# Pool-weight fold one group per block, gate in the output stage, rings set apart, and the next modulation block behind two of six product groups, in a conditioned hybrid layer on one core

## The chip, the cores and the metric

One Trainium2 chip, of which the kernel uses one core. The metric is the device time of one execution in microseconds (us); the numbers shown are single runs and their median.

## The reference

The layer takes x of 4096 tokens by 1024 and a conditioning vector c of 1024, all in float32:

```python
mod = silu(c) @ w_ada + b_ada
shift, scale, gate = split(mod, 3, axis=-1)
h = layer_norm(x) * (1.0 + scale) + shift
proj = h @ w_in + b_in                       # 1024 -> 2560
u_a, z_a, glu_b, z_b = proj[..., :512], proj[..., 512:1024], proj[..., 1024:2048], proj[..., 2048:]
pooled = causal_multiscale_pool(u_a)         # windows 2, 4, 8, 16, one per group of 128, minus u itself
y_a = (einsum("bsgc,gcd->bsgd", pooled, w_pool) + b_pool) * ls_pool * silu(z_a)
v = glu_b[..., :512] * sigmoid(glu_b[..., 512:])
v = silu(layer_norm(causal_depthwise_conv(v, w_dw, b_dw)) * ln_conv_g + ln_conv_b)   # 31 taps
y_b = (v @ w_pw + b_pw) * silu(z_b)
y = concat(y_a, y_b) @ w_out + b_out
out = layer_norm(ALPHA * x + gate * y) * ln_post_g + ln_post_b
```

Since the pooling is linear in the channels' place, `w_pool` (times `ls_pool`) can be multiplied into the u columns of `w_in`: this is the *fold*. It is four products of a 128 x 1024 slice of transposed `w_in` with a 128 x 128 group of `w_pool`.

## The kernel before

**The products.** TensorE does each float32 product as three (`mm3`, lines 336 to 339): both operands are split into a high and a low part (`split`, ScalarE casts the high part, VectorE subtracts for the low one), and high x high, high x low and low x high are added up in PSUM. A product is 128 weight columns by 512 tokens. Tokens are worked in eight *blocks* of 512 (`sb` 0 to 7); a *chunk* is 128 columns of `w_in`, and its product over the 1024 rows (k = 0 to 7) takes 24 instructions.

**Phase 1** (lines 461 to 498) makes for each block the eight GLU chunks 8 to 15, two by two (`glus`), and the z chunks 16 and 17 (`z_half`). Its input is xT, x transposed, normalised, scaled and shifted, as high and low part. While block sb is worked, xT of block sb + 1 is prepared: `row_stats` loads four tiles of 128 tokens, takes mean and variance with two ScalarE scans each (lines 265 and 267), transposes the eight columns of statistics on TensorE (`xcp`), copies them to a row (`rowsx`, line 275), writes them to DRAM (`rD`) and reads them back spread over the partitions (`xbc`). `norm_T` loads the transposed x (`xk`, two k at a time) and applies the statistics and the scale on VectorE (lines 292 and 294); `mod_xT` makes the high part on ScalarE (line 303) and the low part on VectorE (line 304) and writes both to DRAM (`xD`). Phase 2 reads them back for the z_a chunks 4 to 7, the u chunks 0 to 3 (with the folded weights) and the chunks 18 and 19. The x tiles, `xbc` and the `xk` tiles share a ring of five buffers, "tm".

**Block 0** is different (lines 374 to 439). Its x is transposed on TensorE (`turn_x`), and its scale and shift come straight from the modulation. `w_ada` is loaded in five pieces; `mod_block` multiplies each into `macc` on VectorE (line 181), adds it up over the partitions on TensorE (line 186) and makes the scale and shift of one or two k. For each k, a row of 128 x 1024 of `w_in` is loaded (`load_row`) and split in two goes (`split_cols`, three column chunks and one), x is made (`mod_turned`, lines 321 to 324), then come the modulation block and the transposes of the next k, and then the products of k for six chunks at once, the *six product groups*: 8, 12, 9, 13, 10, 14. `load_row` keeps its rows in two "wraw" buffers and in the homes of `gate_bc` and `gbo`, which are not filled yet.

**The fold** (`fold_u`, lines 350 to 364) comes after the z chunks of block 0, all four groups one after the other. Each loads `wT` (512 KB), makes eight 128 x 128 products into two PSUM banks (`fv`), copies them out (`wf`), writes them to DRAM (`uD`), and folds the bias (`bu`). `wT` and `wf` use the two "wraw" buffers. The gate (`mod_gate` and lines 490 to 498, eight loads of 512 KB and eight VectorE operations of 1024 columns, two products) comes after block 1.

**The convolution** (`conv`, 31 taps on VectorE, lines 558 to 586) is written after phase 2 but has no place of its own: VectorE's order has its taps between the other steps. The order of each engine is set by a scheduler before the run, from priorities and estimated times; at run time each engine takes its instructions strictly in that order. So does SP, which issues nearly all the DMAs: a load whose buffer isn't free holds up all that stand behind it. After the phases comes the output stage: pointwise product, `w_out` scaled by the gate, and the last layer norm.

Of the kernel before, what the change touches and what calls it, by code (L numbers as in the profile page):

```python
# [17 lines left out]
P = 128  # L18
# [21 lines left out]
def tile_layer(ctx, tc, x, x_t, w_in_t, c, w_ada, b_ada, w_in, b_in, w_pool, b_pool, ls_pool, w_dw, b_dw,  # L40
# [132 lines left out]
    def mod_block(b, k0, nk, wts):  # L173
        w = nk * P
        acc = s2.tile([P, 2, w], F32, tag="bc", bufs=2, name=f"macc_{b}", padded_shape=[P, 2, DH])
        last = None
        for kt in range(KT):
            if kt == 0:
                nc.vector.tensor_scalar(acc, wts[kt], sc[:, 0:1], None, op0=ALU.mult)
            else:  # L180
                last = nc.vector.scalar_tensor_tensor(acc, wts[kt], sc[:, kt : kt + 1], acc,
                                                      op0=ALU.mult, op1=ALU.add)
        ps = tp_bank(f"mod{b}")
        for i in range(2):
            for j in range(nk):
                nc.tensor.matmul(ps[:, nk * i + j : nk * i + j + 1], acc[:, 1 - i, j * P : (j + 1) * P],
                                 ones[:, 0:1], start=True, stop=True)
# [69 lines left out]

    def load_x(i):
        xt = ph.tile([P, D], F32, tag="tm", bufs=5, name=f"x{i}")
        nc.sync.dma_start(xt, tok(xv, i))  # L260
        return xt

    def col_stats(src, n, nmean, rstd, name):
        sm = st.tile([P, 3], F32, tag="sm", bufs=4, name=f"sm{name}")
        nc.scalar.activation(src, src, AF.Identity, accum_out=sm[:, 0:1])  # L265
# [5 lines left out]
    def to_rows(pb, cs, dst, name):  # L271
        n = cs.shape[1]
        transpose(pb[:n, :P], cs)
        rows = st.tile([n, P], F32, tag="rows8", bufs=2, name=f"rows{name}", padded_shape=[4 * TT, P])
        nc.scalar.copy(rows, pb[:n, :P])
        nc.sync.dma_start(dst, rows)

    def row_stats(sb):
        cs = st.tile([P, 8], F32, tag="cs", bufs=2, name=f"xcs{sb}")
        for t in range(TT):  # L280
            i = sb * TT + t
            xt = load_x(i)
            col_stats(xt, D, cs[:, t : t + 1], cs[:, 4 + t : 5 + t], f"x{i}")
# [3 lines left out]
        return bc  # L287

    def norm_T(sb, bc, k):
        z = ph.tile([P, 2, T], F32, tag="tm", bufs=5, name=f"xk{sb}_{k}")  # L290
        nc.sync.dma_start(z, x_t[k * P : (k + 2) * P, sb * T : (sb + 1) * T].rearrange("(k p) s -> p k s", p=P))
        nc.vector.tensor_tensor(z, z, bc[:, 0:1, :].to_broadcast([P, 2, T]), op=ALU.add)  # L292
# [56 lines left out]

    def fold_u(g, wpl):  # L350
        wT = wraw(f"wT{g}")
        nc.sync.dma_start(wT, w_in_t[g * P : (g + 1) * P, :])
        wf = wraw(f"wf{g}")
        for hb in range(2):
            pb = s2_bank(f"fv{g}_{hb}")
            for j in range(4):
# [4 lines left out]
        nc.sync.dma_start(uD[g], wf)  # L361
        pb = s2_bank(f"bu{g}")
        nc.tensor.matmul(pb[:, 0:1], wpl[:, g, :], vec("b_in", g), start=True, stop=True)
# [25 lines left out]
    def load_row(k):  # L389
        home = k % 4  # L390
        rows[k] = (wraw(f"wr{k}") if home < 2 else
                   cst.tile([P, D], F32, tag=("gate", "gbo")[home - 2], name=f"wr{k}"))
        nc.sync.dma_start(rows[k], w_in[k * P : (k + 1) * P, 8 * P : 16 * P])

# [6 lines left out]

    def split_cols(k, m0, m1):
        split(*(t.rearrange("p (h c) -> p h c", h=2)[:, :, m0 * P : m1 * P] for t in (*Wg[k], rows[k])))

# [30 lines left out]
    gate_bc = cst.tile([P, D], F32, tag="gate", name="gate_bc")  # L435
    gbo = cst.tile([P, D], F32, tag="gbo", name="gbo")
    for k in range(KT):
        for i in range(2):
            after(nc.sync.dma_start(xD[k][0][:, i, :], xT[k][i].bitcast(F32)), last, True)

    def glu(sb, m, pa, pg):
# [19 lines left out]
    for sb in range(NSB):  # L461
# [13 lines left out]
        xT_next = mod_xT(sb + 1, zs, 0)  # L475
        zs = norm_T(sb + 1, bc, 4) + norm_T(sb + 1, bc, 6)
        z_half(sb, xT)
        xT = xT_next + mod_xT(sb + 1, zs, 4)
        if sb == 0:
            wpl = s2.tile([P, MC, P], F32, tag="cto", bufs=2, name="wpl")  # L480
# [4 lines left out]
            nc.vector.tensor_tensor(bpl, vec("b_pool", 0, 4), vec("ls", 0, 4), op=ALU.mult)  # L485
            for g in range(MC):
                fold_u(g, wpl)
        if sb == 1:
            mod_gate(gbo)
            gb = wraw("gb")  # L490
            nc.sync.dma_start(gb, b_ada[2 * D : 3 * D].partition_broadcast(P))
            for h in range(2):
                sl = slice(h * 512, (h + 1) * 512)
                gp = tp_bank(f"gp{h}")
                nc.tensor.matmul(gp, ones, gbo[:, sl], start=True, stop=True)
                nc.vector.tensor_tensor(gate_bc[:, sl], gp, gb[:, sl], op=ALU.add)
            nc.sync.dma_start(gbo, b_out.partition_broadcast(P))
            nc.vector.tensor_tensor(gbo, gbo, gate_bc, op=ALU.mult)
# [13 lines left out]
    for sb in range(NSB):  # L512
# [188 lines left out]
    def out_tile(sb, t, ys):  # L701
# [104 lines left out]
```

## Time and profile before

| what | us |
|---|---|
| runs | 1396.62, 1403.74, 1404.29 |
| median | 1403.74 |
| the profiled execution | 1397.84 |
| its span | 1395.8 |
| TensorE busy in it | 1356.4 (97%) |
| VectorE busy | 1193.9 (86%) |
| ScalarE busy | 432.6 (31%) |

A row of a timeline gives start, duration, engine, line, operation, output and inputs, shape, the count of instructions run together, and in brackets how long the engine had been idle before it and what ended that. Times are in us from the start of the span. PE is TensorE, DVE is VectorE, ACT is ScalarE, SPq the queue of SP. The granted clock is the share of full speed that TensorE had.

### The profile page before, as it was taken

To read this page: it belongs to the slowest core of one execution; us is meant where nothing else is said; L and a number is where in the kernel's file an instruction comes from. 1 tells how busy PE (TensorE), PEld (TensorE's weight loads), DVE (VectorE), ACT (ScalarE), POOL (GpSimd) and SP (SyncE) were. 2 spreads that over 40 slices of the span, in tenths; PEclk is the share of its full clock that TensorE was granted. 3 is DMA by queue.
4 is the path that set the end of the run, shared out by engine and by line. 5 is a ranking of instruction groups with operands and counts; after the bars stand their busy time and mean duration, and the time that the engine had idled before them with its cause. 6 is when DMAs were issued, how large, how long until landed. Compare 5 with 4: busy or idle time off the path is not lost.

```text
span 1395.8 us, 17137 instructions
## 1 busy us (share of the span) xinstructions
PE 1356.4 (97%) x6045; PEld 1118.5 (80%) x6045; DVE 1193.9 (86%) x2348; ACT 432.6 (31%) x772; POOL 131.0 (9%) x193
## 2 busy tenths in 40 slices
PE   4898999999999999999999999999999999999997
PEld 3777888888888888888888888888888888888886
DVE  8688989983569999899899699999997899998754
ACT  3544235245531231411114111343234131322310
POOL 1000000010100001210111110100111101001111
PEclk9999999999999999999999999999999999999999
DMA  9958677477563662360541723466444443433511
GB/s 323 328 180 323 214 275 267 163 267 235 180 249 124 226 194 83 131 233 23 182 139 59 234 67 123 131 203 196 157 167 148 139 159 118 162 129 130 186 61 76
DMA packets 113352, 243.81 MB, mean 175 GB/s; under 512 B 15027, under 2 KB 45555, under 8 KB 113267
## 3 DMA queue, kind: packets, MB, share of 16 engines
q1 hardware_dynamic: 103984, 209.15, 43.4%
q0 software_dynamic: 9216, 33.56, 7.2%
q8 instruction: 47, 0.77, 0.2%
q14 instruction: 39, 0.31, 0.1%
q10 hardware_dynamic: 66, 0.02, 0.0%
HBM read 156.65 MB, written 86.04 MB: 174 GB/s over the span
## 4 chain that ended last, share of the span: by engine, by line
PE 90%; DMA 5%; DVE 2%; ACT 2%; SPq 1%; issue 1%; DVEq 0%; ACTq 0%
PE po L713 25%; PE p L338 6%; PE p L339 6%; PE p L337 6%; PE p2z L338 4%; PE p2u L338 4%; PE p2z L337 4%; PE p2z L339 4%; PE p2u L337 4%; PE p2u L339 4%; PE pw L689 2%; PE pw L691 2%; PE pw L690 2%; PE p2b L338 2%; PE p2b L337 2%; PE p2b L339 2%
## 5 line engine op out<-in xcount | busy, mean ns | idle before, releaser
L576 DVE SCALAR_TENSOR_TENSOR cx<-cv,wdw,cx 128x513 f32<-128x513 f32 (+1 forms) x240 | 145.7, 613 | 0.7
L576 DVE SCALAR_TENSOR_TENSOR ca<-cx,wsum,ca 128x256 f32<-128x256 f32 (+1 forms) x240 | 143.7, 611 | 0.1
L576 DVE SCALAR_TENSOR_TENSOR ca<-cv,wdw,ca 128x256 f32<-128x256 f32 (+1 forms) x224 | 134.3, 611 | 0.0
L742 POOL TENSOR_TENSOR ors<-ove,mhalf 128x1 f32<-128x1 f32 x32 | 46.9, 1467 | 408.8 <-DVE ove L738 400.4
L736 ACT ACTIVATE ojk<-r,osm 128x1024 bf16<-128x1024 f32 x31 | 35.6, 1148 | 148.3 <-DVE osm L733 148.3
L332 POOL DMA_DIRECT2D x2r<-xD x64 | 34.8, 544 | 402.8 <-PE p2b L339 276.7
L731 DVE SCALAR_TENSOR_TENSOR r<-po,r 128x512 f32<-128x512 f32 x62 | 40.9, 687 | 22.0 <-PE po L713 21.9
L576 DVE SCALAR_TENSOR_TENSOR lx<-lv,wdw,lx 128x257 f32<-128x257 f32 x120 | 57.5, 479 | 0.0
L576 DVE SCALAR_TENSOR_TENSOR la<-lx,wsum,la 128x256 f32<-128x256 f32 x120 | 57.3, 478 | 0.0
L576 DVE SCALAR_TENSOR_TENSOR la<-lv,wdw,la 128x256 f32<-128x256 f32 x112 | 53.3, 478 | 0.0
L269 POOL TENSOR_TENSOR xcs<-smx,mhalf 128x1 f32<-128x1 f32 x28 | 20.7, 740 | 343.9 <-DVE smx L268 343.6
L517 ACT ACTIVATE sz<-p2z,cols 128x512 f32<-128x512 f32 x32 | 22.0, 688 | 95.6 <-PE p2z L339 95.5
L292 DVE TENSOR_TENSOR xk<-xk,xbc 128x1024 f32<-128x1024 f32 x28 | 34.1, 1222 | 17.2 <-DMA xk<-in_x_t_dram 17.2
L303 ACT ACTIVATE x<-xk,shc 128x512 fp32r<-128x512 f32 x56 | 38.0, 719 | 31.5 <-DVE xk L294 31.5
L304 DVE SCALAR_TENSOR_TENSOR x<-xk,shc,x 128x512 fp32r<-128x512 f32 x56 | 40.4, 749 | 8.3 <-ACT x L303 8.3
L524 ACT ACTIVATE u<-p2u,bu 128x512 f32<-128x512 f32 x32 | 22.0, 689 | 70.4 <-PE p2u L339 70.4
L745 DVE SCALAR_TENSOR_TENSOR r<-r,ors,b_bc 128x1024 f32<-128x1024 f32 (+1 forms) x33 | 41.1, 1248 | 3.2 <-POOL ors L742 3.1
L443 ACT ACTIVATE sg<-p,cols 128x512 f32<-128x512 f32 x32 | 21.9, 686 | 70.3 <-PE p L339 69.8
L265 ACT ACTIVATE x<-x 128x1024 f32<-128x1024 f32 x28 | 29.6, 1059 | 40.6 <-DMA x<-in_x_dram 39.7
L713 PE MATMUL po<-wo0h,ya 128*128 128x512 f32 x128 | 41.2, 392 | 0.0
L713 PE MATMUL po<-wo1h,ya 128*128 128x512 f32 x128 | 41.1, 390 | 0.0
L705 DVE SCALAR_TENSOR_TENSOR r<-r,gbo 128x1024 f32<-128x1024 f32 x32 | 39.0, 1218 | 1.7 <-DMA r<-in_x_dram 1.7
(360 smaller groups left out, 4107.4 us busy)
## 6 DMA issues: line engine op xcount, KB each, us to landing
x2r<-xD POOLq DMA_DIRECT2D x64, 512.0 KB, 7.3
xD<-x SPq DMA_DIRECT2D x56, 512.0 KB, 5.4
x<-in_x_dram SPq DMA_DIRECT2D x32, 512.0 KB, 6.8
r<-in_x_dram SPq DMA_DIRECT2D x32, 512.0 KB, 3.6
out_dram<-r SPq DMA_DIRECT2D x31, 512.0 KB, 2.6
xk<-in_x_t_dram SPq DMA_DIRECT2D x28, 512.0 KB, 8.2
wa<-in_w_ada_dram SPq DMA_DIRECT2D x32, 256.0 KB, 6.4
vD<-v SPq DMA_DIRECT2D x32, 256.0 KB, 2.2
```

The lines of the kernel that those rows point to most:

```text
L303: nc.scalar.activation(h2[:, 0, :], z, AF.Identity, bias=shc[:, k : k + 1])
L304: nc.vector.scalar_tensor_tensor(h2[:, 1, :], z, shc[:, k : k + 1], h2[:, 0, :].bitcast(F32), op0=ALU.add, op1=ALU.subtract)
L337: nc.tensor.matmul(ps, w[0], X[0], start=first, stop=False)
L338: nc.tensor.matmul(ps, w[0], X[1], start=False, stop=False)
L339: nc.tensor.matmul(ps, w[1], X[0], start=False, stop=last)
L576: nc.vector.scalar_tensor_tensor(dst, src, wt, dst, op0=ALU.mult, op1=ALU.add)
L705: xg = nc.vector.scalar_tensor_tensor(r, r, ALPHA, gbo, op0=ALU.mult, op1=ALU.add)
L713: mm = nc.tensor.matmul(po[h], lhs, Wo[k][wi][:, h * 512 : (h + 1) * 512], start=(k == 0 and wi == 0 and lhs is yh), stop=last)
L731: nc.vector.scalar_tensor_tensor(r[:, sl], po[h], 1.0, r[:, sl], op0=ALU.mult, op1=ALU.add, accum_out=sm[:, h : h + 1])
L736: nc.scalar.activation(jk, r, AF.Square, bias=sm[:, 2:3], accum_out=ss)
L742: nc.gpsimd.tensor_tensor(rs, ve, mhalf[:, 0:1], op=ALU.pow)
L745: nc.vector.scalar_tensor_tensor(r[:, sl], r[:, sl], rs, b_bc[:, sl], op0=ALU.mult, op1=ALU.add)
```

## The change

It has six parts.

1. The fold is done one group per block, after blocks 2 to 5, each with its `wT` loaded one block earlier. `wpl` (`w_pool` times `ls_pool`) is prepared after block 1 in the program's text. The folds use the PSUM banks of transposes ("tpb") in place of "s2b", and `wf` lies in the ring "tm".
2. The gate is written in phase 2, after block 2 of it (`GATE_SB`), and `gate_bc` and `gbo` are made only after phase 1.
3. The x tiles for the statistics leave the ring "tm": the four of block 1 are loaded early into "ca" buffers, those of later blocks go by turns into the two homes of `gate_bc` and `gbo`. The writes of block 0's xT to `xD` come after the last `xk` load of block 1 instead of after the last modulation block.
4. `load_row` loads three of the four column chunks of either half; chunks 11 and 15 are loaded behind (`w3r`, eight loads of 128 x 256) and split on their own. The high part of a row is cast before x is made, the low part after. `wzr` goes from "wraw" to the homes of the gate.
5. The modulation block and transposes of the next k come behind two of the six product groups.
6. The rings `sm` and `rows8` are split in one for x and one for the convolution; `bs` has three buffers instead of four.

```diff
-        sm = st.tile([P, 3], F32, tag="sm", bufs=4, name=f"sm{name}")
+        sm = st.tile([P, 3], F32, tag=f"sm{name[0]}", bufs=4, name=f"sm{name}")
...
-        rows = st.tile([n, P], F32, tag="rows8", bufs=2, name=f"rows{name}", padded_shape=[4 * TT, P])
+        rows = st.tile([n, P], F32, tag=f"rows{name[0]}", bufs=1, name=f"rows{name}", padded_shape=[4 * TT, P])
...
-            xt = load_x(i)
+            xt = x_early[t] if sb == 1 else load_x(i, t % 2)
...
-    def fold_u(g, wpl):
-        wT = wraw(f"wT{g}")
-        nc.sync.dma_start(wT, w_in_t[g * P : (g + 1) * P, :])
-        wf = wraw(f"wf{g}")
+    def fold_u(g, wpl, wT):
+        wf = ph.tile([P, D], F32, tag="tm", bufs=5, name=f"wf{g}")
         for hb in range(2):
-            pb = s2_bank(f"fv{g}_{hb}")
+            pb = tp_bank(f"fv{g}_{hb}")
...
     for k in range(KT):
+        hi, lo = (both(t)[:, :, : 3 * P] for t in Wg[k])
+        nc.scalar.copy(hi, rows[k])
         xT.append(mod_turned(pb, k))
-        split_cols(k, 0, 3)
-        split_cols(k, 3, 4)
-        if k + 1 < KT:
-            if k + 1 in starts:
-                b = starts[k + 1]
-                last = mod_block(b, *mods[b], wad[b])
-            pb = turn_x(xt_next, k + 1)
-        for n0, ps in zip(first, pss0):
+        nc.vector.tensor_tensor(lo, rows[k], hi.bitcast(F32), op=ALU.subtract)
+        for i, (n0, ps) in enumerate(zip(first, pss0)):
+            if i == 2 and k + 1 < KT:
+                if k + 1 in starts:
+                    b = starts[k + 1]
+                    last = mod_block(b, *mods[b], wad[b])
+                pb = turn_x(xt_next, k + 1)
             mm3(ps, W[n0][k], xT[k], k == 0, k == KT - 1)
+    for q in range(2):
+        raw = wraw(f"w3r{q}").rearrange("p (k h c) -> p k h c", k=4, h=2)
+        for k in range(4):
+            nc.sync.dma_start(raw[:, k], both(w_in[(4 * q + k) * P : (4 * q + k + 1) * P, 8 * P : 16 * P])[:, :, 3 * P :])
+        for k in range(4):
+            hi, lo = (both(t)[:, :, 3 * P :] for t in Wg[4 * q + k])
+            split(hi, lo, raw[:, k])
...
+        if sb == 0:
+            for k in range(KT):
+                for i in range(2):
+                    after(nc.sync.dma_start(xD[k][0][:, i, :], xT[k][i].bitcast(F32)), x_loads[1])
         z_half(sb, xT)
         xT = xT_next + mod_xT(sb + 1, zs, 4)
-        if sb == 0:
+        if sb == 1:
...
-            for g in range(MC):
-                fold_u(g, wpl)
-        if sb == 1:
-            mod_gate(gbo)
...
+        if 1 <= sb <= MC:
+            wT = wraw(f"wT{sb - 1}")
+            nc.sync.dma_start(wT, w_in_t[(sb - 1) * P : sb * P, :])
+        if 2 <= sb <= MC + 1:
+            fold_u(sb - 2, wpl, wTs.pop(0))
+        if 1 <= sb <= MC:
+            wTs.append(wT)
...
+        if sb == GATE_SB:
+            mod_gate(gbo)
```

Three places show how the order of instructions moves. The first is TensorE at the end of the z chunks of block 0 (`p1z_1`), before; `fv` and `bu` are the fold, `p_1_8` and the like the products of block 1 for chunk 8 with x of k = 0, `x_1_0`.

```order
L339 MATMUL p1z_1_1016<-x_0_7_741,wz1l 128x512
L358 MATMUL fv_0_1069<-wpl,wT_1066 128x128 x4
L358 MATMUL fv_1_1075<-wpl,wT_1066 128x128 x4
L363 MATMUL bu_1082<-cols,wpl 128x1
L337 MATMUL p_1_8_1192<-x_1_0_962,wg0h 128x512
L337 MATMUL p_1_12_1193<-x_1_0_962,wg0h 128x512
L337 MATMUL p_1_9_1247<-x_1_0_962,wg0h 128x512
L337 MATMUL p_1_13_1248<-x_1_0_962,wg0h 128x512
L358 MATMUL fv_0_1088<-wpl,wT_1085 128x128 x4
L358 MATMUL fv_1_1094<-wpl,wT_1085 128x128 x4
L363 MATMUL bu_1101<-cols,wpl 128x1
L358 MATMUL fv_0_1107<-wpl,wT_1104 128x128 x4
```

The same place of the changed kernel, where lines 344 to 346 are the three products; `xcp_1101` transposes statistics of block 2.

```order
L346 MATMUL p1z_1_1024<-x_0_7_736,wz1l 128x512
L74 MATMUL xcp_1101<-ident,xcs_1068 8x128
L344 MATMUL p_1_8_1118<-x_1_0_954,wg0h 128x512
L344 MATMUL p_1_12_1119<-x_1_0_954,wg0h 128x512
L344 MATMUL p_1_9_1173<-x_1_0_954,wg0h 128x512
L345 MATMUL p_1_8_1118<-x_1_0_954,wg0h 128x512
L346 MATMUL p_1_8_1118<-x_1_0_954,wg0l 128x512
L345 MATMUL p_1_12_1119<-x_1_0_954,wg0h 128x512
```

The folds are gone from here: three products with x's high part follow the z chunks, and the fourth is the first that reads its low part.

The second place is VectorE between the first normalising operation of block 1 (`xk_0`, line 292, some rows above these) and the low half of `x_1_0` (line 304), before; lines 570 to 576 are the convolution.

```order
L292 TENSOR_TENSOR xk_4_978<-xk_4_978,xbc_880 128x1024
L294 SCALAR_TENSOR_TENSOR xk_0_882<-xk_0_882,s_281,xbc_880 128x512 x2
L576 SCALAR_TENSOR_TENSOR ca_0_6445<-cv_0_6444,wdw,ca_0_6445 128x256
L576 SCALAR_TENSOR_TENSOR ca_0_6445<-cx_0_6446,wsum,ca_0_6445 128x256
L292 TENSOR_TENSOR xk_6_983<-xk_6_983,xbc_880 128x1024
L576 SCALAR_TENSOR_TENSOR ca_1_6502<-cx_1_6503,wsum,ca_1_6502 128x256
L294 SCALAR_TENSOR_TENSOR xk_2_887<-xk_2_887,s_281,xbc_880 128x512 x2
L576 SCALAR_TENSOR_TENSOR cx_1_6503<-cv_1_6501,wdw,cx_1_6503 128x257
L576 SCALAR_TENSOR_TENSOR ca_1_6502<-cv_1_6501,wdw,ca_1_6502 128x256
L576 SCALAR_TENSOR_TENSOR cx_0_6446<-cv_0_6444,wdw,cx_0_6446 128x257
L294 SCALAR_TENSOR_TENSOR xk_4_978<-xk_4_978,s_281,xbc_880 128x512 x2
L304 SCALAR_TENSOR_TENSOR x_1_0_962<-xk_0_882,shc,x_1_0_962 128x512
```

In the changed kernel the stretch from behind `xk_0`'s addition and one tap is this, with the lines 299, 301, 311 and 604 for 292, 294, 304 and 576, and `v_3` (line 462) the GLU of block 0's last chunk:

```order
L604 SCALAR_TENSOR_TENSOR cx_0_6456<-cv_0_6454,wdw,cx_0_6456 128x257
L604 SCALAR_TENSOR_TENSOR ca_0_6455<-cv_0_6454,wdw,ca_0_6455 128x256
L299 TENSOR_TENSOR xk_2_879<-xk_2_879,xbc_872 128x1024
L301 SCALAR_TENSOR_TENSOR xk_0_874<-xk_0_874,s_281,xbc_872 128x512 x2
L604 SCALAR_TENSOR_TENSOR ca_0_6455<-cx_0_6456,wsum,ca_0_6455 128x256
L604 SCALAR_TENSOR_TENSOR cx_0_6456<-cv_0_6454,wdw,cx_0_6456 128x257
L299 TENSOR_TENSOR xk_4_970<-xk_4_970,xbc_872 128x1024
L462 SCALAR_TENSOR_TENSOR v_3_951<-p_0_11_899,cols,sg_3_949 128x512
L604 SCALAR_TENSOR_TENSOR ca_0_6455<-cv_0_6454,wdw,ca_0_6455 128x256
L301 SCALAR_TENSOR_TENSOR xk_2_879<-xk_2_879,s_281,xbc_872 128x512 x2
L299 TENSOR_TENSOR xk_6_975<-xk_6_975,xbc_872 128x1024
L311 SCALAR_TENSOR_TENSOR x_1_0_954<-xk_0_874,shc,x_1_0_954 128x512
```

The four additions still come ahead of the first low half, with fewer taps of the convolution between them.

The third place is SP's queue ahead of block 1's statistics (`rD_270`, `xbc_872`) in the changed kernel. `x_1069` and the next three are the x tiles of block 2 in the two gate homes, `wT_1442` and `wT_1812` fold weights.

```order
L504 DMA lsb<-in_ls_pool_dram 128x512
L509 DMA wT_1442<-in_w_in_t_dram 128x1024
L265 DMA x_1069<-in_x_dram 128x1024
L265 DMA x_1077<-in_x_dram 128x1024
L265 DMA x_1085<-in_x_dram 128x1024
L503 DMA wpl<-in_w_pool_dram 128x4x128
L265 DMA x_1093<-in_x_dram 128x1024
L463 DMA vD_0_165<-v_0_886 128x512
L509 DMA wT_1812<-in_w_in_t_dram 128x1024
L281 DMA rD_270<-rowsx_869 8x128
L463 DMA vD_0_173<-v_1_891 128x512
L593 DMA cv_0_6454<-vD_0_165 128x2x256
```

Before it was this; `rowsx_877` is the row of block 1's statistics, line 439 writes block 0's x.

```order
L439 DMA xD_0_149<-x_0_6_709 128x512 x2
L260 DMA x_859<-in_x_dram 128x1024
L260 DMA x_867<-in_x_dram 128x1024
L439 DMA xD_0_157<-x_0_7_741 128x512
L482 DMA wpl<-in_w_pool_dram 128x4x128
L439 DMA xD_0_157<-x_0_7_741 128x512
L446 DMA vD_0_165<-v_0_894 128x512
L565 DMA cv_0_6444<-vD_0_165 128x2x256
L446 DMA vD_0_173<-v_1_899 128x512
L446 DMA vD_0_181<-v_2_904 128x512
L565 DMA cv_1_6501<-vD_0_173 128x2x256
L276 DMA rD_270<-rowsx_877 8x128
```

The x loads of block 2 and two fold weights now stand ahead of the write of block 1's statistics, in place of block 1's own x loads and the writes of block 0's x.

More of the change, by code (lines that the diff above doesn't have):

```diff
@@ L34 @@
 EARLY = 2
+GATE_SB = 2
 PERSB = (1, 1, 1, 1, 1, 1, 0, 0)
@@ L256, in tile_layer, with load_x @@
     ph = ph_ctx.enter_context(tc.tile_pool(name="ph1", bufs=1, reuse_waits="tile"))
-    def load_x(i):
-        xt = ph.tile([P, D], F32, tag="tm", bufs=5, name=f"x{i}")
+    def load_x(i, home=None):
+        if home is None:
+            xt = ph.tile([P, D], F32, tag="tm", bufs=5, name=f"x{i}")
+        else:
+            xt = cst.tile([P, D], F32, tag=("gate", "gbo")[home], name=f"x{i}")
         nc.sync.dma_start(xt, tok(xv, i))
@@ L391, in load_row, with both @@
         rows[k] = (wraw(f"wr{k}") if home < 2 else
-                   cst.tile([P, D], F32, tag=("gate", "gbo")[home - 2], name=f"wr{k}"))
-        nc.sync.dma_start(rows[k], w_in[k * P : (k + 1) * P, 8 * P : 16 * P])
+                   cst.tile([P, D], F32, tag=("gate", "gbo")[home - 2], name=f"wr{k}"))[:, : 6 * P].rearrange(
+                       "p (h c) -> p h c", h=2)
+        nc.sync.dma_start(rows[k], w_in[k * P : (k + 1) * P, 8 * P : 16 * P].rearrange(
+            "p (h c) -> p h c", h=2)[:, :, : 3 * P])
+    def both(t):
+        return t.rearrange("p (h c) -> p h c", h=2)
     mods = ((0, 1), (1, 1), (2, 2), (4, 2), (6, 2))
@@ L400, in tile_layer @@
             load_row(k)
-    def split_cols(k, m0, m1):
-        split(*(t.rearrange("p (h c) -> p h c", h=2)[:, :, m0 * P : m1 * P] for t in (*Wg[k], rows[k])))
+    x_early = []
+    for t in range(TT):
+        xt = s2.tile([P, D], F32, tag="ca", bufs=6, name=f"x{TT + t}", padded_shape=[P, 2 * (HQ + T + 1)])
+        nc.sync.dma_start(xt, tok(xv, TT + t))
+        x_early.append(xt)
     xT = []
@@ L424, in tile_layer @@
     for q in range(2):
-        raw = wraw(f"wzr{q}")
+        raw = cst.tile([P, D], F32, tag=("gate", "gbo")[q], name=f"wzr{q}")
         nc.sync.dma_start(raw.rearrange("p (k n) -> p k n", k=4),
@@ L434, in tile_layer @@
             W[16 + m].append((Wz[k // 4][0][:, a : a + P], Wz[k // 4][1][:, a : a + P]))
[L435 to L439, printed above, removed]
     def glu(sb, m, pa, pg):
@@ L485, in tile_layer @@
             nc.vector.tensor_tensor(bpl, vec("b_pool", 0, 4), vec("ls", 0, 4), op=ALU.mult)
-            for g in range(MC):
-                fold_u(g, wpl)
-        if sb == 1:
-            mod_gate(gbo)
[L490 to L498, printed above, removed]
+        if 1 <= sb <= MC:
[5 more added lines that the diff above has]
+            wTs.append(wT)
     ph_ctx.close()
     lt = pool("lt", reuse_waits="tile")
+    gate_bc = cst.tile([P, D], F32, tag="gate", name="gate_bc")
+    gbo = cst.tile([P, D], F32, tag="gbo", name="gbo")
     ph_ctx = ExitStack()
@@ L554, in tile_layer @@
             nc.sync.dma_start(zD[1][sb][:, m - 2, :], sz)
+        if sb == GATE_SB:
+            mod_gate(gbo)
+            gb = wraw("gb")
+            nc.sync.dma_start(gb, b_ada[2 * D : 3 * D].partition_broadcast(P))
+            for h in range(2):
+                sl = slice(h * 512, (h + 1) * 512)
+                gp = tp_bank(f"gp{h}")
+                nc.tensor.matmul(gp, ones, gbo[:, sl], start=True, stop=True)
+                nc.vector.tensor_tensor(gate_bc[:, sl], gp, gb[:, sl], op=ALU.add)
+            nc.sync.dma_start(gbo, b_out.partition_broadcast(P))
+            nc.vector.tensor_tensor(gbo, gbo, gate_bc, op=ALU.mult)
     ph_ctx.close()
```

15 lines of the change are left out of this document (9 added, 6 removed).

## The prediction

> **What bounds the kernel now.** I read the page's busy shares first, then a table of stages, then the list of waits, then single rows around the places that this table points to. One line of the page and the table (us; TensorE, its weight load, VectorE, ScalarE, GpSimd; then granted clock, DMA share, GB/s):
>
> ```profile
> PE 1356.4 (97%) x6045; PEld 1118.5 (80%) x6045; DVE 1193.9 (86%) x2348; ACT 432.6 (31%) x772; POOL 131.0 (9%) x193
> ...
> 0.00:20.46 20.46, 2.52 (x11) 1.93 (x11) 13.81 (x47) 8.48 (x10) 4.16 (x37) 1.00 0.94 293
> 20.46:71.42 50.96, 44.72 (x201) 36.07 (x202) 35.77 (x75) 26.07 (x43) 1.10 (x2) 0.97 1.00 336
> 71.42:93.50 22.08, 22.08 (x100) 18.14 (x99) 19.28 (x48) 7.17 (x12) 1.62 (x2) 1.00 0.61 206
> 93.50:114.80 21.30, 14.53 (x65) 12.88 (x63) 21.02 (x39) 10.18 (x18) 0.00 (x0) 0.68 0.64 201
> ...
> 122.00:370.00 248.00, 248.00 (x1106) 204.12 (x1105) 202.10 (x383) 100.31 (x160) 16.34 (x21) 1.00 0.70 247
> 370.00:1388.60 1018.60, 1017.34 (x4538) 839.38 (x4536) 894.89 (x1743) 277.10 (x526) 106.84 (x130) 1.00 0.42 145
> ```
>
> TensorE is the bound. From 122 to 1388.6 us it is busy for 1265.34 of 1266.60 us, so nothing in that stretch can be won except by fewer products, and the change keeps their number. What can be won lies before 122 us: the start up to the first product (20.46), the products of block 0 (6.24 us idle of 50.96), and the stretch 93.50 to 114.80, where TensorE is idle for 6.77 us and runs at a clock of 0.68. The list of TensorE's waits (total, times, longest) has the same places at its head:
>
> ```profile
> PE mod L186 <- DVE macc L181: 11.4, 2, 9.5
> PE fv L358 <- DMA wT<-in_w_in_t_dram: 4.8, 2, 4.5
> ```
>
> The 9.5 us lie before the first product; the rest of the first line lies in block 0 and comes back below.
>
> **The pool-weight fold leaves the boundary of blocks 0 and 1.** TensorE's rows there (start, duration, and in brackets the idle time before and its releaser):
>
> ```profile
> 82.61 0.39 PE L337 MATMUL p1z<-x,wz0h 128*128 128x512 f32 x1
> ...
> 93.26 0.40 PE L339 MATMUL p1z<-x,wz1l 128*128 128x512 f32 x1
> 93.50 1.95 PE L358 MATMUL fv<-wpl,wT 128*128 128x128 f32 x16
> 95.28 0.33 PE L363 MATMUL bu<-cols,wpl 128*128 128x1 f32 x2
> 97.62 2.07 PE L337 MATMUL p<-x,wg0h 128*128 128x512 f32 x4 [2.01 <-ACT x L303]
> 99.96 3.75 PE L358 MATMUL fv<-wpl,wT 128*128 128x128 f32 x16 [0.27 <-DMA wT<-in_w_in_t_dram]
> ...
> 108.42 3.76 PE L358 MATMUL fv<-wpl,wT 128*128 128x128 f32 x16 [4.49 <-DMA wT<-in_w_in_t_dram]
> 111.83 0.77 PE L338 MATMUL p<-x,wg0h 128*128 128x512 f32 x1
> 112.40 0.63 PE L339 MATMUL p<-x,wg0l 128*128 128x512 f32 x1
> 112.83 0.63 PE L338 MATMUL p<-x,wg0h 128*128 128x512 f32 x1
> 113.25 0.63 PE L339 MATMUL p<-x,wg0l 128*128 128x512 f32 x1
> 113.68 1.05 PE L337 MATMUL p<-x,wg1h 128*128 128x512 f32 x2
> 114.53 0.43 PE L338 MATMUL p<-x,wg0h 128*128 128x512 f32 x1
> ```
>
> A product at full clock costs 0.227 us: the 48 of the z chunks take from 82.61 to 93.50. A fold with the clock full costs 2.0 us (1.95 and the `bu` behind it). So 93.50 to 114.80 holds three folds (6.0) and eleven products (2.5), 8.5 us of work in 21.3 us. The loss is **12.8 us**: idle time and half clock. The four folds themselves remain as work; they only move, one each into blocks 2 to 5.
>
> At their new places each weight tile `wT` is loaded a block earlier, and a block is 240 products, 54 us, against the some 4.5 us that TensorE waited for such a load. I cost the four folds at nothing over their 2.0 us. The cover is that block of lead; without it, 4.5 us each, as in the row at 108.42.
>
> **What is late next at that boundary.** Without the fold TensorE goes straight from the z chunks to block 1, whose first products need x of block 1. The high half comes from ScalarE, the low half from VectorE, and after three high-half products the next one needs the low half. The rows of that chain before:
>
> ```profile
> 73.30 1.25 ACT L443 ACTIVATE sg<-p,cols 128x512 f32<-128x512 f32 x2
> ...
> 80.72 0.26 ACT L275 COPY rowsx<-xcp 8x128 f32<-8x128 f32 x1 [5.05 <-PE xcp L73]
> ...
> 90.26 1.23 DVE L292 TENSOR_TENSOR xk<-xk,xbc 128x1024 f32<-128x1024 f32 x1
> 91.40 0.49 DVE L576 SCALAR_TENSOR_TENSOR ca<-cv,wdw,ca 128x256 f32<-128x256 f32 x1
> ...
> 96.05 1.42 DVE L294 SCALAR_TENSOR_TENSOR xk<-xk,s,xbc 128x512 f32<-128x512 f32 x2
> ...
> 103.93 0.76 DVE L304 SCALAR_TENSOR_TENSOR x<-xk,shc,x 128x512 fp32r<-128x512 f32 x1
> ```
>
> From the statistics' row copy to the first normalising operation were 9.5 us (80.72 to 90.26). In the new order VectorE has, from that operation to the end of the first low half, four wide additions, six operations of 512 columns and six convolution taps. An operation starts 0.09 us before the one ahead of it ends (90.26 + 1.23 against 91.40), so they cost 1.14, about 0.66 (1.42 for the pair) and 0.40: 4.6 + 4.0 + 2.4 = 11.0 us. Before it was 14.4 (90.26 to 103.93 + 0.76). The row copy no longer waits for its transpose, which now stands before block 0's last pair of chunks; it stands on ScalarE behind the third of the three sigmoids, which ended at 74.55 before, and behind scans of three x tiles of block 2, one of them loaded into a home that the first scan has to free. I place it at 77: bounds 74.6 (right behind the sigmoids) and 80.7 (as before). The first low half is then ready at 77 + 9.5 + 11.0 = 97.5. TensorE is ready for it at 93.5 − 1.0 (the start, below) + 0.7 (three products) = 93.2. The new stall is **4.3 us**, by the bounds 1.9 to 8.0; a quicker load could make it nothing, since part of the 9.5 us was VectorE being busy with convolution.
>
> After it the clock may be halved. Before, it was half in 97.52 to 104.35 and in 107.76 to 114.59, and full where two idle times of 1.85 and 2.18 us stood close together:
>
> ```profile
> 46.00:56.00 10.00, 5.96 (x28) 4.39 (x27) 6.01 (x14) 8.85 (x14) 0.55 (x1) 1.00 1.02 375
> ...
> 97.52:104.35 6.83, 6.04 (x22) 5.07 (x22) 6.83 (x13) 3.23 (x8) 0.00 (x0) 0.50 0.40 146
> ```
>
> So a half-clock stretch costs between nothing and 3.4 us (half of 6.83). I take the middle, **1.7 us**.
>
> The Trainium skill ("TensorE: Matmul & The Clock Gate", Part 1: The HAM clock gate) says that the clock falls to half after at least one idle window of about 3.4 us and is full again after as long of work. The trace agrees only in part: it was halved right after an idle time of 2.01 us, which had only the short fold products around it. By that page a stall of under 3.4 us would cost no half clock, and the sum would be 1.7 us lower.
>
> **The start.** In block 0 the modulation block and the transposes of the next k now follow two of six product groups, so six products, 1.36 us, move in front of the wait for `macc` (1.82 us); that is a gain of up to 1.36, as long as the next x isn't needed sooner. That wait, the waits around the product of k = 4, and the operations that the change moves there:
>
> ```profile
> 32.02 1.30 PE L186 MATMUL mod<-ones,macc 128*128 128x1 f32 x8 [1.82 <-DVE macc L181]
> ...
> 50.17 1.66 PE L337 MATMUL p<-x,wg4h 128*128 128x512 f32 x6 [1.85 <-ACT x L321]
> 54.02 0.50 PE L338 MATMUL p<-x,wg4h 128*128 128x512 f32 x1 [2.18 <-DVE x L324]
> ...
> L196 DVE TENSOR_TENSOR wg4l<-wr,wg4h x2: 421/690/960, 42.3 to 43.2; 128x768 fp32r<-128x768 f32 x1, 128x256 fp32r<-128x256 f32 x1
> ...
> L195 ACT CAST wg4h<-wr x2: 401/619/837, 41.4 to 42.2; 128x768 fp32r<-128x768 f32 x1, 128x256 fp32r<-128x256 f32 x1
> ...
> L265 ACT ACTIVATE x<-x 128x1024 f32<-128x1024 f32 x28 | 29.6, 1059 | 40.6 <-DMA x<-in_x_dram 39.7
> ...
> L267 ACT ACTIVATE x<-x,xcs x28: 1134/1141/1157, 50.0 to 375.4; 128x1024 f32<-128x1024 f32 x28
> ```
>
> The fourth column chunk's splits leave this place: four VectorE operations of 0.42 (−1.7 us ahead of that low half). In exchange ScalarE gets one more scan and both squares of block 1's early tiles ahead of its x: 1.06 + 2 × 1.14 less three casts of 0.40, +2.1 us. Their balance is +0.4, so the start gains **1.0 us**, with bounds of a 3.1 gain and a 0.7 loss. The smaller weight loads free DMA time in a stretch where the DMA share is 1.00, but four tiles of x are loaded there instead; I count nothing.
>
> **The gate.** Its eight VectorE operations, with their eight loads on SP's queue, move from about 140 us to the end of phase 1:
>
> ```profile
> L147 DVE SCALAR_TENSOR_TENSOR gbo<-wag,sc,gbo x7: 1272/1276/1281, 140.0 to 180.7; 128x1024 f32<-128x1024 f32 x7
> ...
> 320.00:400.00 80.00, 79.39 (x356) 64.95 (x355) 26.19 (x55) 40.72 (x75) 6.60 (x12) 1.00 0.60 205
> ```
>
> That is 10 us, in a stretch where VectorE was busy for 26 of 80 us and the DMA share was 0.60; convolution moved earlier fills part of that hole. The cover is this room, and three buffers each for u and its gate. I take nothing: bounds −0.6 (the one wait of that stretch goes) and +2 (as one wait on an x low half at 54.02). The rings set apart, three buffers for `bs` instead of four (VectorE uses them in order) and the later writes of `xD` (first read in phase 2) cost nothing by the same view: TensorE waits for none of them.
>
> **The sum.** −12.8 − 1.0 + 4.3 + 1.7 = **−7.8 us**. The profiled execution took 1397.84 us, 1395.8 of it the span; it gives 1390.0. The runs were 1396.62, 1403.74 and 1404.29: with the profiled one, two near 1397 and two near 1404, and I know no reason for it. The median, 1403.74, would give 1395.9. I forecast from the mean of the four, 1400.6: **1392.8 us**. What a measurement of this kernel can tell from no change is 0.5%, 7.0 us: faster is under 1396.7, slower over 1410.8.
>
> **The rivals.**
>
> *B: the stall takes the fold's place.* If block 1's x is as late as it was behind the fold, 12.8 us come back as waiting and only the start's 1.0 stays: 1399.6, no change. It needs the row copy at about 84 or later. For it: the copy's write stands in SP's queue behind a fold weight's load that waits for VectorE, and behind x loads that wait for ScalarE's scans. Against it: that is 9 us after the end of the sigmoids before (74.55), and between the first of them and the copy ScalarE has only one scan, of 1.06 us.
>
> *C: no stall.* If the loads land in less than 6 us, x is there in time: 1400.6 − 12.8 − 1.0, and up to the start's 3.1 us: 1386.8 to 1384.7. For it: the 9.5 us contain convolution work that now stands elsewhere.
>
> *D: slower, by the two homes of x.* From block 2 on, the four x tiles of a block go through two homes instead of a ring of five. The third load waits in SP's queue for ScalarE's second scan of the first, and everything behind it on SP waits too: the statistics' write, `xbc`, `xk`, `vD`. A block's chain becomes longer by a load and two scans:
>
> ```profile
> x<-in_x_dram SPq DMA_DIRECT2D x32, 512.0 KB, 6.8
> ```
>
> 6.8 + 1.06 + 1.14 = 9.0 us, six times. It decides from where less than 6.5 us of the 9.0 are hidden: 2.5 × 6 = 15, more than the 7.8 gained by 7. With half hidden the six cost 27: 1420. Against it: the order has these loads nearly a block, 54 us, ahead of their use.
>
> *E: the change doesn't do what it says:* the fold's wait goes with it to blocks 2 to 5 (4 × 4.5 us, less the 12.8 and 1.0): 1400.6 + 4.2 with the new stall 1410.8.
>
> **How the numbers follow.** Forecast (1387 to 1399) 0.58, of which 0.45 under 1396.7 and 0.13 over; B 0.16, no change; C 0.14, faster; D 0.07, slower; E 0.05, 0.03 of it no change and 0.02 slower. Faster 0.59, same 0.32, slower 0.09. The range runs from C, 1384, to just over B and the cost bounds of the forecast (stall 8.0, half clock 3.4, gate 2), 1403.
>
> **What would show it.** Right: in the list of waits `fv <- wT` is gone; between 91 and 100 us TensorE waits once, for VectorE's low half of x, for 2 to 8 us; then it runs without a gap to 370. Wrong: a wait of over 8 us there (B), none (C), one at every block's beginning from block 2 (D), or one of some 4.5 us before each fold (E). The start's step is wrong if block 0's products don't end by 71 us, the gate's if TensorE waits around 380 to 420 us.

## The result and the profile after

The changed kernel takes **1389.19 us** (median of five, 1385.91 to 1390.93), the kernel before 1403.74 (five, 1396.62 to 1404.47): a ratio of 0.9899, 95% interval 0.987 to 0.9929. The profiled execution took 1390.93 us, 6.9 less than the one before; the medians differ by 14.6, because the profile of before was one of its quick executions and that of after the slowest of the five. The waits of TensorE after:

```profile
PE mod L189 <- DVE macc L182: 10.8, 2, 10.0
PE p L345 <- DVE x L331: 5.0, 3, 3.9
PE vpsa L74 <- DMA vrowsa<-in_b_in_dram: 3.0, 1, 3.0
PE p L344 <- ACT wg0h L428: 2.6, 1, 2.6
PE cps L74 <- POOL corr L135: 2.3, 1, 2.3
PE p L344 <- ACT x L328: 2.0, 2, 1.7
PE p L345 <- DVE x L311: 1.8, 1, 1.8
```

The waits for `wT` are gone; line 331 is the low half of block 0's x, line 311 that of block 1's. The stages after (columns as before):

```profile
20.46:71.42 50.96, 42.97 (x186) 33.96 (x187) 35.55 (x77) 31.17 (x53) 3.91 (x4) 0.93 0.85 274
71.42:91.50 20.08, 20.08 (x90) 16.28 (x90) 11.17 (x32) 9.24 (x17) 2.23 (x4) 1.00 0.88 289
91.50:104.50 13.00, 11.18 (x43) 8.68 (x42) 13.00 (x21) 6.84 (x10) 0.00 (x0) 0.87 1.01 349
...
120.00:370.00 250.00, 250.00 (x1142) 207.37 (x1141) 239.02 (x461) 106.58 (x175) 19.29 (x22) 1.00 0.62 219
320.00:400.00 80.00, 80.00 (x375) 66.56 (x374) 77.28 (x119) 22.24 (x33) 0.00 (x0) 1.00 0.56 200
```

At the boundary of blocks 0 and 1, 1.82 us are idle in place of 6.77: one wait, for VectorE's low half of x, just under the 2 to 8 us that the prediction named. From 120 to 370 us TensorE runs without a gap, and it doesn't wait at 380 to 420. The start is worse: 7.99 us idle in place of 6.24, at a lower clock. Block 0's product groups end at about 75 us instead of 71.4, which by the prediction's own sign makes its step on the start wrong. VectorE's hole at 320 to 400 is filled, and the one wait there is gone. The rows of the places that the prediction named, TensorE, then ScalarE and VectorE:

```profile
29.85 1.67 PE L344 MATMUL p<-x,wg1h 128*128 128x512 f32 x6 [1.74 <-ACT x L328]
32.29 1.05 PE L189 MATMUL mod<-ones,macc 128*128 128x1 f32 x8 [0.77 <-DVE macc L182]
...
53.78 0.80 PE L345 MATMUL p<-x,wg4h 128*128 128x512 f32 x1 [3.89 <-DVE x L331]
...
67.71 0.50 PE L345 MATMUL p<-x,wg6h 128*128 128x512 f32 x1 [0.87 <-DVE x L331]
...
97.09 0.94 PE L344 MATMUL p<-x,wg0h 128*128 128x512 f32 x3
99.85 0.50 PE L345 MATMUL p<-x,wg0h 128*128 128x512 f32 x1 [1.82 <-DVE x L311]
...
77.65 0.24 ACT L280 COPY rowsx<-xcp 8x128 f32<-8x128 f32 x1
...
88.81 1.23 DVE L299 TENSOR_TENSOR xk<-xk,xbc 128x1024 f32<-128x1024 f32 x1 [0.53 <-DMA xk<-in_x_t_dram]
...
99.05 0.75 DVE L311 SCALAR_TENSOR_TENSOR x<-xk,shc,x 128x512 fp32r<-128x512 f32 x1
```

And two windows:

```profile
52.88:59.70 6.82, 5.92 (x14) 4.72 (x15) 3.67 (x10) 6.82 (x17) 0.55 (x1) 0.50 0.77 239
...
100.66:104.08 3.42, 3.42 (x10) 2.65 (x9) 3.42 (x7) 1.38 (x2) 0.00 (x0) 0.50 0.91 216
```

The clock was halved from the last 0.9 us of the wait at k = 4 on, and again behind the wait for block 1's x.

### The profile page after: what moved, and what is told of

It reads as the page before. It is cut to its first block, busy times and chain, and to the rows that moved or that the text cites. A ratio compares the mean times of both kernels' runs of the same rounds, so it can differ in the third digit from the quotient of the medians.

```text
span 1389.1 us, 17150 instructions
## 1 busy us (share of the span) xinstructions
PE 1353.5 (97%) x6045; PEld 1115.3 (80%) x6045; DVE 1193.2 (86%) x2348; ACT 433.2 (31%) x772; POOL 135.0 (10%) x193
## 4 chain that ended last, share of the span: by engine, by line
PE 93%; DMA 3%; DVE 1%; ACT 1%; SPq 1%; issue 0%; DVEq 0%; ACTq 0%
PE po L741 25%; PE p L345 7%; PE p L346 7%; PE p L344 7%; PE p2z L344 4%; PE p2z L346 4%; PE p2u L346 4%; PE p2u L344 4%; PE p2z L345 4%; PE p2u L345 4%; PE pw L719 2%; PE pw L718 2%; PE pw L717 2%; PE p2b L346 2%; PE p2b L344 2%; PE p2b L345 2%
## 5 line engine op out<-in xcount | busy, mean ns | idle before, releaser
L604 DVE SCALAR_TENSOR_TENSOR cx<-cv,wdw,cx 128x257 f32<-128x257 f32 (+1 forms) x240 | 146.5, 619 | 0.4
L274 POOL TENSOR_TENSOR xcs<-smx,mhalf 128x1 f32<-128x1 f32 x28 | 23.6, 848 | 260.7 <-DVE smx L273 212.3
L197 ACT CAST yb<-z 128x512 fp32r<-128x512 f32 x32 | 19.8, 618 | 69.5 <-DVE z L724 59.4
```

Of the source, the lines that this page charges most:

```text
L604: nc.vector.scalar_tensor_tensor(dst, src, wt, dst, op0=ALU.mult, op1=ALU.add)
```

## The experiments

There are twelve runs in three sets; the kernels of a set and the kernel before ran on the same chip. Medians of one set are compared with each other, since the kernel before scattered from 1393.9 to 1411.3.

**First set.** Beside the kernel before (median 1404.42) ran the changed kernel again, the fold moved alone, the fold put back, and an attempt at the start.

*The changed kernel again,* unaltered: 1390.19 (1386.47 to 1392.71).

> The changed kernel once more, unaltered, beside the others. Its five executions were 1385.9, 1387.0, 1389.2, 1390.2 and 1390.9. Theory: the spread is TensorE's clock alone; an execution of about 1386 has neither or only one of the two half-clock stretches (52.9 to 59.7 and 100.7 to 104.1, together worth 5.1 us) that the one of 1390.9 has, with the same waits. Rival: the waits themselves differ between executions.

Its profile is of the slowest execution too, 1392.71, with the same waits (3.88 at k = 4, 2.6 for block 1's x) and the same two half-clock stretches. The theory on the spread thus wasn't put to the test.

*The fold alone,* in the kernel before:

```diff
-            for g in range(MC):
-                fold_u(g, wpl)
+        if 2 <= sb <= MC + 1:
+            fold_u(sb - 2, wpl, wTs.pop(0))
```

> The kernel before with part 1 alone: one fold group per block behind blocks 2 to 5, its weights loaded a block ahead; nothing else changed. Theory: the fold hid the lateness of block 1's x, so taking it away alone uncovers a wait. The row copy of the statistics stays at about 80.7 us, the first normalising operation at about 90; the new order puts four additions, eight operations of 512 columns, about ten convolution taps and one gate operation between that and the first low half, some 15.5 us, so TensorE waits from about 94.2 to 106, 11 to 12 us, with a half-clock stretch behind it: 12.8 less 11.6 less 1.7, no change (within 3 us of before). Rival: the fold alone brings its whole 12.8 us (about 0.991 of before).

Measured 1421.89, 1.0132 of before [1.0097, 1.0166]: slower. The wait it uncovers is there, in two rows of TensorE and one of VectorE in between:

```profile
101.93 2.08 PE L337 MATMUL p<-x,wg0h 128*128 128x512 f32 x4 [7.25 <-ACT x L303]
110.05 0.79 PE L338 MATMUL p<-x,wg0h 128*128 128x512 f32 x1 [6.04 <-DVE x L304]
...
103.82 1.28 DVE L147 SCALAR_TENSOR_TENSOR gbo<-wag,sc,gbo 128x1024 f32<-128x1024 f32 x1
```

These are 13.3 us, about what the fold's departure was to save (12.8), and the gate's operations now stand between those that make x. Another 13.9 us arise at 967 us, at the start of the output stage: ScalarE's cast of `ya` (966.39) had waited 8.1 us for its load, which SP issued at 962.98, right after VectorE had finished at 962.87 with a `cbc` tile, one of the two buffers of its ring. A wait of 3.5 us at 988 follows. These two make up the whole difference from before, 17.5 us; without them the fold alone would be about as slow as before, as the theory had it. That the edit reached the output stage by way of the scheduler's order is an inference. The rival, 12.8 us gained by the fold alone, is out.

*The fold put back* behind block 0 in the changed kernel (the same edit reversed, with its buffers and banks as before):

> The changed kernel with the fold of all four groups put back behind block 0; the other parts stay. Theory: the 1.8 us wait for x is filled by the first fold group, but the three loads in the two weight buffers and the half clock come back: 8 to 12 us slower than the changed kernel, so within 4 us of before. Rival, that the gain came from the start and the queues and not from the fold: within 3 us of the changed kernel.

Measured 1385.27 (1383.74 to 1387.64), 0.9873 of before [0.9842, 0.9905], and 4.9 under the changed kernel of the same set. My theory falls: the fold stands where it stood and TensorE waits for nothing.

```profile
93.06 1.95 PE L365 MATMUL fv<-wpl,wT 128*128 128x128 f32 x16
...
111.32 1.95 PE L365 MATMUL fv<-wpl,wT 128*128 128x128 f32 x16
...
94.19 0.75 DVE L311 SCALAR_TENSOR_TENSOR x<-xk,shc,x 128x512 fp32r<-128x512 f32 x1
```

```profile
93.50:125.00 31.50, 31.50 (x158) 26.65 (x157) 31.50 (x74) 15.72 (x28) 1.37 (x2) 1.00 1.01 386
```

The first low half of block 1 comes at 94.9 instead of 104.7 before; the first fold group covers the rest, and the other groups come between products that are ready, when their weights have landed. In this profile the start is quicker too, by 4.0 us (the fold begins at 93.06, where the changed kernel's z chunks end at 97.09), with the same order of instructions there: at k = 4 ScalarE's scan did not wait for its tile, and TensorE waited 1.95 instead of 3.89.

*Scans later* at the start of the changed kernel:

```diff
+        if behind is not None:
+            after(scan, behind)          # tiles 0, 1: hs of k = 4; tiles 2, 3: hs of k = 5
```

> The changed kernel with one order added: ScalarE's first scans of block 1's four early x tiles come behind the second half of x for k = 4 (two tiles) and k = 5 (two tiles). Theory: the third scan's wait for its tile holds up the low half of x for k = 4, TensorE's 3.9 us wait at 49.9 to 53.8 and the half clock behind it (6.8 us at half, 3.4 us); with the scans behind, that wait falls under 1 us and block 0's products end by 68 us: 3 to 7 us less than the changed kernel, of which the boundary of block 1 may eat 2. Rival: the low half of k = 4 waits for the last modulation pieces or the weight row in any case, and the wait stays over 3 us: within 1.5 us of the changed kernel.

Measured 1398.68, 8.5 over the changed kernel: a miss. The wait at k = 4 goes, and others take its place:

```profile
PE p L351 <- DVE x L337: 5.0, 3, 3.6
PE p L351 <- DVE x L315: 3.6, 1, 3.6
...
PE p L350 <- ACT sg L466: 1.7, 1, 1.7
```

The 3.6 of line 337 now stands at k = 6, and behind it ScalarE's work is late: block 1's row copy comes at 79.98 instead of 77.65, and the wait for block 1's low half is 3.6 instead of 1.8. That the wait at k = 4 left with the scan confirms what held it; the price of moving the scan was left out of the theory.

**Second set** (before 1397.35, without the changed kernel; the run with the modulation back is its nearest): which part lets block 1's x come in time.

*x alone,* in the kernel before:

```diff
+            xt = x_early[t] if sb == 1 else load_x(i)
...
+                    after(nc.sync.dma_start(xD[k][0][:, i, :], xT[k][i].bitcast(F32)), x_loads[1])
```

> The kernel before with the half of part 3 that concerns block 1 alone: its four x tiles for the statistics are loaded early into buffers of their own, and block 0's x is written to DRAM behind the loads of block 1's x; the fold stays behind block 0, all four groups, and everything else is as before. New theory, from the run with the fold put back: the 12.8 us were lost because block 1's x came late (first low half at 104.6 us) and the fold's loads stood in the queue behind its chain, and not because the fold stood there; the statistics made early bring the first low half to about 95, and TensorE has a product to do wherever a fold weight is missing. Then this alone gives 10 to 18 us less than before (0.987 to 0.993). First theory, that the fold has to leave: no more than 3 us less.

Measured 1393.98 (nine executions at 1393 to 1395, three at 1404 to 1405), 0.9984 [0.996, 1.0008]: no difference shown. Half right: the boundary is clear (31.50 of 31.50 us busy from 93.5 to 125, the row copy at 69.78), and the same loss comes back at block 3, two rows of TensorE and a window:

```profile
217.38 2.07 PE L339 MATMUL p<-x,wg0h 128*128 128x512 f32 x4 [6.17 <-ACT x L305]
222.61 0.79 PE L340 MATMUL p<-x,wg0h 128*128 128x512 f32 x1 [3.15 <-DVE x L306]
```

```profile
213.91:227.56 13.65, 7.02 (x16) 5.05 (x17) 13.65 (x21) 5.48 (x8) 0.00 (x0) 0.50 0.64 218
```

9.3 us idle and 13.65 at half clock, right behind the gate, whose last operations VectorE did at 184 to 204 us.

*No early x* in the changed kernel (block 1's tiles back in the ring of five):

> The changed kernel with block 1's four x tiles back in the ring of five and not loaded ahead; all else as changed. New theory (x early is the cause): the statistics, the row copy and the first low half come 3 us or more later, TensorE waits 5 us or more at the boundary with a half-clock stretch behind it, and without the early scans the low half of k = 4 comes sooner: together 3 to 10 us slower than the changed kernel. First theory (the fold's place is the cause): within 3 us of the changed kernel, or faster by the start.

Measured 1395.47: 6.9 over the run with the modulation back, 5 to 6 over the changed kernel's medians in the other comparisons, within what was expected. The wait for the first low half is 2.9 us, though, less than the theory's 5 or more; TensorE also waits 1.0 for the statistics, and k = 4 is little better (3.1 for the high half instead of 3.9 for the low one). Some 2 us of the loss are there before the boundary: the z chunks end at 99.14 instead of 97.07.

*The gate back* in phase 1, and with it the later x tiles in the ring of five:

> The changed kernel with the gate back behind block 1, as before, and so the x tiles of blocks 2 to 7 in the ring of five instead of the two homes. Forecast's step: the gate's place is worth nothing (within 3 us of the changed kernel). New theory: the scans of block 2, which stood ahead of block 1's row copy because of the two homes, now stand behind it, and the first low half has three additions and no convolution tap ahead of it instead of four and six: it comes some 5 us sooner, the wait of 1.8 to 2.6 us goes and so does the half clock at 101: 2 to 5 us faster than the changed kernel, if VectorE makes up for the gate later.

Measured 1404.56, 16.0 over the run with the modulation back: both expectations missed. Three new waits:

```profile
157.68 0.79 PE L345 MATMUL p<-x,wg0h 128*128 128x512 f32 x1 [5.12 <-DVE x L311]
...
335.38 0.50 PE L345 MATMUL p<-x,wg0h 128*128 128x512 f32 x1 [3.12 <-DVE x L311]
...
510.73 0.74 PE L344 MATMUL p2z<-x2r,w4h 128*128 128x512 f32 x1 [4.63 <-ACT sg L463]
```

*The modulation back* ahead of all six groups (`i == 0` for `i == 2`):

> The changed kernel with the next modulation block and transposes ahead of all six product groups again. Forecast's step: its place behind two groups is worth up to 1.4 us at the wait for the sums of k = 2 and 3 (0.8 us in the changed kernel, 1.8 before): 0 to 2 us slower than the changed kernel. Rival: with the transposes sooner, x of the next k comes sooner too, and the waits at k = 1 (1.7 us) and k = 4 (3.9 us) shrink by 1.4 us each: 1 to 6 us faster.

Measured 1388.59, within the changed kernel's scatter: no difference shown. The wait for `macc` is 0.79 as against 0.77, so the new place isn't what shortened it.

**Third set** (before 1405.17): the change put together anew.

*x and gate:* the kernel before with block 1's x early, the gate in phase 2 and the rings apart.

> The kernel before with three things: block 1's four x tiles early and block 0's x written later (as in the run with x alone), the gate in phase 2, and the rings apart; the x tiles of blocks 2 to 7 stay in the ring of five, the fold behind block 0, rows and modulation as before. Theory: x early clears the boundary of block 1 (done in the run with x alone), and the gate in phase 1 was what made block 4's x late there (9.4 us of wait and 6.8 us of lost clock around 214 us); with the gate gone from phase 1 both are gone, and the start is the better one of the run with x alone: 1380 to 1386. Rival: the late x around 214 came from the ring of five, in which the x tiles wait for x of the block before; then that wait stays, 5 us or more, and the time is 1390 or more.

Measured 1391.74, 5.7 over the range expected. The wait around 214 is gone. The rings were apart with the gate back as well, and it waited at 157, which points to the gate and not to the rings; the gate moved with the rings joint wasn't run. Two smaller ones remain, at the places where they were with the gate back:

```profile
324.80 0.50 PE L340 MATMUL p<-x,wg0h 128*128 128x512 f32 x1 [2.38 <-DVE x L306]
...
494.04 0.73 PE L339 MATMUL p2z<-x2r,w4h 128*128 128x512 f32 x1 [2.44 <-ACT sg L446]
```

*With the two homes* for later x tiles as well:

> As the kernel of the run with x early and the gate moved, and the x tiles of blocks 2 to 7 in the two gate homes, as in the changed kernel. Theory: the scans of block 2 now stand ahead of block 1's row copy on ScalarE and cost the chain some 2 to 3 us there, hidden behind the first fold group; within 3 us of the run without homes, or 2 to 6 us slower if ScalarE's extra scans around k = 6 and 7 hold x up. If the ring of five was the cause at 214 us, faster by 8 or more.

Measured 1387.98, 3.8 under the run without the homes, a gain of a size that none of the expectation's cases named. Both waits are gone, though block 1's row copy comes at 75.68 instead of 70.99.

*And the fold spread:*

> As the kernel with x early, the gate moved and the two homes, and the fold spread over blocks 2 to 5: the changed kernel without the split rows and without the modulation's new place. Theory: the fold's place costs what the first fold group covers at the boundary of block 1: 2 to 6 us slower than with the fold behind block 0. Rival (forecast): the spread is worth something by itself, it is faster.

Measured 1391.14, 3.2 slower, as the theory has it: TensorE waits 3.6 us for block 1's low half, with 6.8 us at half clock behind it.

*Whole rows* in the changed kernel:

> The changed kernel with whole rows of four column chunks loaded and split at once again (no second loads of 128 x 256). Theory: part 4 costs at the start: eight small casts and two operations more per k on ScalarE, which is the engine that x of k = 4 and k = 6 waits for, and eight loads of 512 bytes a row that hold up the early x tiles. Without it the wait at k = 4 (3.9 us) and the half clock behind it go: 3 to 7 us faster than the changed kernel. Rival: the whole rows fill the DMA queues at the start and the rows of k = 2 to 5 come later: 1 to 4 us slower.

Measured 1388.85 (five executions from 1384.0 to 1391.5, whose median is 1388.46, and one of 1962.5 at a mean clock of 0.657, which stays unexplained): no difference shown from the changed kernel's 1389.19 and 1390.19, which were measured in other sets. The wait at k = 1 is gone, that at k = 4 fell to 2.57, and block 1's first product came 2.7 us sooner (94.40 instead of 97.09), but a wait of 3.5 us came up for the second `macc`, and behind the wait for block 1's x (2.6) 6.8 us ran at half clock.

## Why the prediction was right, and where it wasn't

The time lay in the range, 3.6 us under the forecast; between the two profiled executions the forecast was 0.9 off (1390.0 for 1390.93). That nearness is partly luck: the start came out 4.6 us worse than forecast and the boundary 2.5 better, and the main step had the wrong cause. By the medians the change moved the time by 14.6 us, nearly twice the 7.8 that was forecast from the rows of a quick execution of before. The executions of before near 1404 weren't profiled, so about half of the medians' difference has no explanation in the rows. In the second set, where before ran mostly quick (1397.35), the nearest kernel was 8.8 under it.

*The fold's departure, 12.8 us.* The loss at its place did go. But it was no price of the fold's place: with the fold alone moved, 13.3 us of waiting stood there instead and nothing was gained; the fold put back is 4.9 faster, the spread added to the rest 3.2 slower. The loss was block 1's x coming at 104.7, with only fold groups left to do, whose weights stood in SP's queue. The step "what is late next" treated x's lateness as something uncovered by the change; it was the cause. What cleared it is part 3: with x alone, and the fold where it was, the boundary has no wait and the first low half comes at 89.8. Which half of that part does it, the early tiles or the later writes of block 0's x, no run separates; without the early tiles the changed kernel lost 5 to 7 us, some 2 of them ahead of the boundary. What the prediction costed at nothing, the gate, keeps this from coming back: with the gate in phase 1 the wait appears at block 3 (9.3 us in x alone) or block 2 (5.1 in the changed kernel). The homes take two further waits of 2.4 us, so rival D had their sign wrong: they make block 1's chain some 5 us longer and the later ones safe.

*The new stall, 4.3 us.* Measured 1.8 and, in the second profile, 2.6. The chain was sized well: row copy 77.65 (77), from first normalising operation to the low half's end 11.0 (11.0), in between 11.2 (9.5). The row copy's place was partly luck: it stands behind the sigmoids, which were late because the start was; with the fold put back, and a quicker start, it came at 74.42. x was ready at 99.8 instead of 97.5, and TensorE at 98.0 instead of 93.2, because of the start. The boundary's loss was thus 3.5 us (1.8 and 1.7), forecast at 6.0.

*The half clock, 1.7 us.* 3.4 us at half speed, 1.7. The rule of the Trainium skill that was weighed there ("TensorE: Matmul & The Clock Gate", Part 1) has an idle window of about 3.4 us for that; here again the clock fell after 1.82 us of idle time.

*The start, a gain of 1.0.* It lost 3.6 us (the z chunks' end at 97.07 against 93.50). The gain costed there, up to 1.36 by the modulation's place, didn't come. TensorE already had six products of k = 1 ahead of the modulation before the change; this row of before stands right ahead of the wait of 1.82, as the same row of after (29.85) does ahead of the 0.77:

```profile
28.54 1.66 PE L337 MATMUL p<-x,wg1h 128*128 128x512 f32 x6 [0.39 <-ACT x L321]
```

The wait for `macc` is 1.05 shorter only because these products began 1.3 us later: `macc` was ready at 32.02 before and at 32.29 after. And with the modulation's place undone it stayed at 0.79. Together the two lost 0.3. Beside this a low half at k = 1 lost 0.3, k = 4 0.1, k = 6 0.9, and the clock some 1.3: behind the one wait of 3.89 at k = 4, 5.9 us of work ran at half speed, where before it was 3.4 us, behind the wait for `macc` (32.8 to 36.2). That is 2.9 of the 3.6; the rest is spread over the stage. The balance at k = 4 was costed well (+0.4). The step that failed counted the modulation's move as a gain and left out the waits at k = 1 and k = 6, and the clock. At k = 1 ScalarE's x waited for the shift:

```profile
27.17 0.96 DVE L430 TENSOR_TENSOR wg2l<-wr,wg2h 128x768 fp32r<-128x768 f32 x1 [0.84 <-ACT wg2h L428]
...
29.02 0.78 ACT L328 ACTIVATE x<-xt,shc,s 128x512 fp32r<-128x512 f32 x1 [0.85 <-DVE shc L192]
```

VectorE made that shift, `shc`, at 28.77 instead of 26.97, behind the low part of row 2. With whole rows VectorE's order is another one, and the wait is gone; the early scans have no part in it, since the first ran at 40.81. At k = 6 VectorE waited 2.46 us for `hs`, which ScalarE did behind the x of k = 7, whose transposes it waited for. Why the third scan's tile lands 2 us later in the changed kernel than with the fold put back, behind the same queue, stays open.

*The gate's place, nothing.* At its new place it costs nothing, as forecast: no wait at 380 to 420, the one wait of 0.6 gone. What its leaving phase 1 is worth wasn't in the sum, since before no wait stood there. With the gate back in the changed kernel the wait of 5.1 and 5 us at half clock behind it make 7.7 us, in x alone the waits of 9.3 have 13.65 at half clock beside them.

Open stays why executions of one kernel differ by 5 us. The recorded mean clocks of the five fit half-clock stretches (0.997 for the two at 1386 to 1387, 0.993 to 0.995 for the others), but no profile of a quick execution of the changed kernel shows which are missing.

A kernel that beats both is the changed one with the fold put back: 1385.27 against 1390.19 and 1404.42 in one set. By the profiles 3.5 to 4.3 us of it are the boundary (a wait of 1.8 to 2.6 and 1.7 of half clock).

## What to carry to other kernels

Before costing work out of a stage, ask what that stage would do without it: here the work that seemed to make TensorE wait was filling a wait for data, and the remedy was to bring the data sooner. An engine that is busy off the critical path (VectorE's gate, 10 us) sets when the next block's input is ready, so a wait cleared at one block comes back at a later one unless that load moves as well. A transfer or scan that is brought forward lands in a stage that was already short of the same engine, and its price belongs in that stage's sum.

## What the runs showed of the hardware

The clock is halved in stretches of 3.41 us or multiples of it (3.42, 6.82, 13.65), and waits of under 2 us were enough (1.82 in the changed kernel), where one of 1.95 us at k = 4 with the fold put back was not:

```profile
48.00:56.00 8.00, 5.79 (x29) 4.34 (x27) 3.75 (x11) 7.92 (x16) 1.10 (x2) 1.00 1.08 328
```

The clock of that window is 1.00 throughout. Likewise waits of 1.74 and 0.77 us close together left it full at 28 to 32 us of the changed kernel, where before one of 1.82 us (30.20 to 32.02) had 3.4 us at half behind it. What decides between the two, the runs don't show.
